# Short and unread products put between runs of 256-column and 512-column products on the tensor engine

## The chip, the cores and the metric

The kernel runs on one core of one Trainium2 chip. The metric is the device time of one launch in microseconds (us). A core has a tensor engine (PE, with its weight loads shown apart as PEld), a vector engine (DVE), a scalar engine (ACT), GpSimd (POOL), a sync engine (SP) that here only issues transfers, and 16 DMA engines.

## The reference

One layer of a hybrid block on 256 latent tokens and 256 context tokens of width 2048, all in float32:

```
mod = silu(c) @ w_ada + b_ada;  shift, scale, gate = split(mod, 3)
h  = rmsnorm(x) * (1 + scale) + shift            # and hc likewise from ctx
xa, za, xb, zb, cv, cg, zc, gl = split(h @ w_in) # widths 7 x 1024 and 3 x 2048
ya = bidirectional gated linear scan of conv4(xa), latents starting from the context's last state
yb = (mean over windows 2, 4, 8, 16 - itself) @ w_pool, per group of 256 channels
yc = silu(layernorm(conv31(cv * sigmoid(cg)))) @ w_pwc + b
t  = sum over k of sigmoid(gl_k) * ((y_k * silu(z_k)) @ w_bout_k)
out = rmsnorm(x + gate * (t @ w_out + b_out)) * final_g
```

Of the context only its `xa` is computed. Nearly all the arithmetic is the products with `w_in`, `w_bout`, `w_pwc` and `w_out`.

## The kernel before

Weights come in pieces of 1 MB (128 partitions of 2048 float32) through three slots. A piece is split into a high part (ACT, L84) and a low part (DVE, L85 through the helper at L210), both of the type float32r, in two halves of 1024 columns each; four buffers of each part let the splits run up to two pieces ahead. The tokens were split in the same way before (`hH`, `hL`). A float32 product is then three float32r products: high by high, high by low, low by high.

`steps` (L297 to L348) is a fixed list of work, one piece of weights each, and sets the order of everything: "xa" and then groups of "xb" and "zb" with the pooling, "cv" and "cg", "gl" and "bout" pairs, "za", "zc", "pwc", and at the end "out". In a step of all kinds but "out", `columns` (L243) takes the weights as the stationary operand, 128x128 at a time, and the tokens as the moving one, 256 columns wide (512 in "xa", where context tokens are taken along): sixteen times L249 and L250 in turn, then sixteen times L253. That is 48 products a step, each with a weight load of its own. "out" (L1065) takes tokens as the stationary operand and 512 columns of weights as the moving one.

Between steps, `Background` emits pieces of elementwise chains into the program, by an estimate of the vector engine's load. Some of them have products of their own, which so come to stand between the runs of `columns`:

- `products` in `lru` (L584): six products of 512 columns for the recurrent gates, through `mm3` (L239 to L241);
- `pool_end` (L808): twelve products of 256 columns of the pooling mixer, also through `mm3`;
- the two sums of the layer norm, 256 columns in plain float32 (L731, L745), and the four of the gate chunks, 512 columns in plain float32 (L940). A plain float32 product shows as two products in the trace.

PE works through all of this in the order in which it is written. Results go to a ring of six banks of PSUM (`bank`) or one of two (`small_bank`).

Of the kernel before, what the change touches and what calls it, by code (L numbers as in the profile page):

```python
# [23 lines left out]

# column offsets inside the packed per-channel vectors
V_G, V_BSH, V_BSC = 0, 16, 32
# [6 lines left out]

# arena offsets (float32 per partition)
A_SQ0, A_XT, A_H, A_S, A_RAW = 0, 8192, 16384, 17408, 17920
# [11 lines left out]
class Feed:  # L47
    """Weight pieces of 8 KB per partition: loaded ahead into slots, and split into two float32r parts."""

# [41 lines left out]
class Background:  # L91
    """Elementwise chains cut into small steps that fill the vector engine between weight splits.

    A chain is a list of named generators that run one after another. Each yields None after what it has just
    emitted, "S" where the next part has to wait for the next weight piece, or a function that says whether the
    next part may be emitted (in a tuple where that is only better so)."""

# [7 lines left out]
    def _step(self, chain):  # L105
        """Emits the next part; False if it can't be emitted yet."""
        if chain["until"] is not None:
            if not chain["until"]():
                return False
            chain["until"] = None  # L110
        try:
            r = next(chain["parts"][0][1])
        except StopIteration:
            self.done.add(chain["parts"].pop(0)[0])
            if not chain["parts"]:
                self.chains.remove(chain)
            return True
        chain["soft"] = isinstance(r, tuple)
        if chain["soft"]:
            r = r[0]  # L120
        if callable(r):
            chain["until"] = r
        return r != "S"
# [22 lines left out]
def hybrid_block_kernel(  # L146
# [91 lines left out]
    def mm3(ps, sh, sl, mh, ml, start, stop):  # L238
        T.matmul(ps, sh, mh, start=start, stop=False)  # L239
        T.matmul(ps, sh, ml, start=False, stop=False)  # L240
        T.matmul(ps, sl, mh, start=False, stop=stop)  # L241

    def columns(jobs):  # L243
        """Sums over k of weights (stationary) times tokens (moving) in three float32r products each; those
        with the low part of the weights come last, so that it may be late. A job: output, high and low parts
        of the weights per k, high and low parts of the tokens per k."""
        for ps, wh, wl, mh, ml in jobs:
            for k in range(len(wh)):
                T.matmul(ps, wh[k], mh[k], start=k == 0, stop=False)  # L249
                T.matmul(ps, wh[k], ml[k], start=False, stop=False)  # L250
        for ps, wh, wl, mh, ml in jobs:
            for k in range(len(wh)):
                T.matmul(ps, wl[k], mh[k], start=False, stop=k == len(wh) - 1)  # L253

    def tiles128(parts):
        """The 128-column tiles of a split piece, high and low."""
        return [[part[i][:, P * k:P * (k + 1)] for part in parts for k in range(8)] for i in range(2)]

    def rsqrt_newton(o, v, tmp, r):
        """o = 1/sqrt(v): square root, reciprocal, one Newton step."""  # L260
        A.activation(r, v, AF.Sqrt)
        recip(r, r)
        tt(tmp, r, r, ALU.mult)
        tt(tmp, tmp, v, ALU.mult)
        ts(tmp, tmp, -0.5, 1.5)
        tt(o, tmp, r, ALU.mult)

    feed = Feed(nc, whp, wlp)

    # order of the weight pieces  # L270
    main_slots = [(f"m{i}", raws[:, i, :]) for i in range(3)]
# [25 lines left out]
    steps = []  # L297
# [57 lines left out]
    with tc.manual_schedule():  # L355
# [1 line left out]
        cin = sml[:, 0:32]  # L357
# [60 lines left out]
        def keep_warm(n):  # L418
            """Products that nothing reads: the tensor engine's clock halves when it has been idle."""
            for _ in range(n):  # L420
                T.matmul(warm, ones, xT[:, 10, :], start=True, stop=True)

# [1 line left out]
        fold = ar[:, A_XS:A_XS + 512]  # L424
# [35 lines left out]

# [1 line left out]
        xa_ps = [bank() for _ in range(6)] + [small_bank() for _ in range(NXA - 6)]  # L462
# [18 lines left out]

# [1 line left out]
        xap = [ar[:, A_XAP + 518 * t:A_XAP + 518 * (t + 1)].rearrange("p (s l) -> p s l", s=2) for t in range(8)]  # L483
# [12 lines left out]
        gth = [ar[:, A_GTH + 512 * i:A_GTH + 512 * (i + 1)] for i in range(2)]  # L496
        # context halves of the split modulated tokens, free after xa: products' operands of the branches
        cH, cL = hH[:, :, 256:512], hL[:, :, 256:512]
# [11 lines left out]

# [1 line left out]
        nsp, tsp, brh, bih = sml[:, 96:112], sml[:, 112:128], sml[:, 128:144], sml[:, 144:160]  # L512

        def prep():
            """softplus(-lam) = max(-lam, 0) + log1p(exp(-|lam|)); log1p(e) = 2 atanh(e / (2 + e))."""
            lam = vt[:, V_LAM:V_LAM + 16]
# [31 lines left out]
        def conv_a(pr):  # L548
            """Two heads: depthwise convolution of width 4, then the two parts of the result."""
            hd = (2 * pr, 2 * pr + 1)  # L550
# [21 lines left out]
        def lru():  # L572
# [11 lines left out]
            def products(h, d):  # L584
                i = h % 2
                for g in range(2):
                    ps = small_bank()
                    w = slice(128 * g, 128 * (g + 1))
                    mm3(ps.rearrange("p (s l) -> p s l", s=2), wH[:, d, w], wL[:, d, w],
                        uH[:, 2 * i:2 * i + 2, :], uL[:, 2 * i:2 * i + 2, :], True, True)  # L590
                    pss[g] = ps
                if d == 1:
                    lru_at["mm"] += 1
# [128 lines left out]
        def layer_norm():  # L722
# [7 lines left out]
            ps = bank()  # L730
            T.matmul(ps[:, 0:256], ones, tree[:, 0:256], start=True, stop=True)  # L731
            A.activation(mu, ps[:, 0:256], AF.Copy, scale=1.0 / 1024)
            yield "S"
# [10 lines left out]
            ps = bank()  # L744
            T.matmul(ps[:, 0:256], ones, tree[:, 0:256], start=True, stop=True)  # L745
            ts(v, ps[:, 0:256], 1.0 / 1024, EPS)
            A.activation(r, v, AF.Sqrt)
# [32 lines left out]

# [1 line left out]
        G.memset(ar[:, A_XAP:A_XAP + 4144], 0.0)  # L782
# [15 lines left out]
        def silu_parts(ps):  # L798
            """(1 + tanh(z / 2)) z, twice silu(z)."""
            th = take("th", th_t)  # L800
# [7 lines left out]
        def pool_end(g):  # L808
# [4 lines left out]
            for j in range(2):  # L813
                for k in range(2):
                    mm3(ps[:, 256 * j:256 * (j + 1)], wH[:, k, 128 * j:128 * (j + 1)],
                        wL[:, k, 128 * j:128 * (j + 1)], pH[:, k, :], pL[:, k, :], k == 0, k == 1)
            for j in range(2):
                t = 2 * g + j
# [53 lines left out]
        def merge_end(k, j):  # L872
            """Two channel tiles of a branch into the sum; after the last branch, half the sum in two parts."""
            a = acc[:, j, :]
# [29 lines left out]
        def gate_chunk(n):  # L904
            """The gate on every partition: silu(c) times the weight rows of each partition, then the sum over
            the partitions; and x + gate * b_out."""
            c = slice(512 * n, 512 * (n + 1))
# [31 lines left out]
            ps = bank()  # L939
            T.matmul(ps, ones, g, start=True, stop=True)  # L940
            A.copy(g, ps)
            yield "S"
# [28 lines left out]
        def finish(t, halves):  # L971
            """The last chunk of a token tile, then the RMS norm over its rows; the first three chunks are
            multiplied by final_g already."""
            var, r, tmp = [sml[:, 16 + 4 * t + i:17 + 4 * t + i] for i in range(3)]
# [25 lines left out]

# [1 line left out]
        first, later, post = [], [], []  # L1002
        step_no = [0]
        avail = load["V"]
        for kind, key, item, q in steps:
# [34 lines left out]
            elif kind == "bout":  # L1040
# [12 lines left out]
                later.append((si + 1, lambda k=k, j=j: merge_end(k, j)))  # L1053
            elif kind == "out":
                if q == 0:
                    if key == 0:
# [8 lines left out]
                def out_mm(t, ps, lo, hi, qs, low):  # L1065
                    """One token tile: tokens stationary, weights moving; the low part of the weights last."""
                    tk = slice(P * t, P * (t + 1))
# [60 lines left out]
def _layout(inputs):  # L1128
    """Arrays in the order in which the kernel reads them: permutations, slices and concatenations only."""
    f = {k: np.asarray(v, dtype=np.float32) for k, v in inputs.items()}  # L1130
# [58 lines left out]
```

## Time and profile before

| | |
|---|---|
| median of 3 runs | 991.86 us (988.95 to 993.12) |
| span of the profiled execution, first to last instruction | 990.5 us |
| own time of the profiled execution, around the span | not given by the profile |
| PE busy | 965.3 us, 97% |
| PE weight loads busy | 893.6 us, 90% |
| DVE busy | 743.6 us, 75% |
| ACT busy | 493.0 us, 50% |
| DMA | 220.70 MB, mean 223 GB/s |

The profile is one execution. Busy shares are averages over the span; PE products are pipelined, so the busy time of one (from its start to its modelled end) is longer than the distance to the start of the next, and how fast PE works is read from the starts. The tensor engine's granted clock is shown as PEclk, 1.00 being the full 2.4 GHz. The first 163 us are the modulation and "xa"; from there to 892 us stand the steps of `columns` with 256 columns; the rest is "out".

### The profile page before, as it was taken

To read this page: it belongs to the slowest core of one execution; us is meant where nothing else is said; L and a number is where in the kernel's file an instruction comes from. 1 tells how busy PE (TensorE), PEld (TensorE's weight loads), DVE (VectorE), ACT (ScalarE), POOL (GpSimd) and SP (SyncE) were. 2 spreads that over 40 slices of the span, in tenths; PEclk is the share of its full clock that TensorE was granted. 3 is DMA by queue.
4 is the path that set the end of the run, shared out by engine and by line. 5 is a ranking of instruction groups with operands and counts; after the bars stand their busy time and mean duration, and the time that the engine had idled before them with its cause. 6 is when DMAs were issued, how large, how long until landed. Compare 5 with 4: busy or idle time off the path is not lost.

```text
span 990.5 us, 18090 instructions
## 1 busy us (share of the span) xinstructions
PE 965.3 (97%) x7528; PEld 893.6 (90%) x7528; DVE 743.6 (75%) x1143; ACT 493.0 (50%) x641; POOL 40.6 (4%) x74
## 2 busy tenths in 40 slices
PE   4999999999999999999999999999999999999996
PEld 1566668999999999999999999999999999998885
DVE  5445456866976775889899899896756788998864
ACT  4212226566656767674444533444565464454442
POOL 0000010000100000000000000000002111101000
PEclk9999999999999999999999999999999999999998
DMA  9897854544545555444555545555468789878652
GB/s 373 322 418 313 359 194 162 211 171 167 181 163 182 182 181 178 174 171 170 203 181 176 200 178 191 193 173 175 169 216 342 256 301 331 326 249 303 214 178 85
DMA packets 34722, 220.70 MB, mean 223 GB/s; under 512 B 4128, under 2 KB 4272, under 8 KB 11856
## 3 DMA queue, kind: packets, MB, share of 16 engines
q1 hardware_dynamic: 28080, 195.28, 54.1%
q0 software_dynamic: 6560, 24.26, 7.2%
q8 instruction: 59, 0.97, 0.4%
q14 instruction: 23, 0.19, 0.1%
HBM read 217.43 MB, written 2.10 MB: 222 GB/s over the span
## 4 chain that ended last, share of the span: by engine, by line
PE 96%; DVE 2%; ACT 1%; DMA 1%; issue 0%; ACTq 0%; SPq 0%; DVEq 0%
PE acc L253 24%; PE acc L250 24%; PE acc L249 24%; PE sm L390 3%; PE acc L239 3%; PE acc L1075 3%; PE acc L1077 3%; PE acc L1078 3%; PE acc L240 2%; PE acc L241 2%; DVE ar L210 1%; PE sm L240 1%; PE sm L239 1%; PE sm L241 1%; DMA ar<-in_xt_dram 1%; PE sm L399 0%
## 5 line engine op out<-in xcount | busy, mean ns | idle before, releaser
L249 PE MATMUL acc<-hH,wh 128*128 128x256 f32 (+1 forms) x2000 | 479.2, 282 | 0.0
L250 PE MATMUL acc<-hL,wh 128*128 128x256 f32 (+1 forms) x2000 | 477.7, 281 | 0.0
L84 ACT CAST wh<-raws 128x1024 fp32r<-128x1024 f32 (+1 forms) x288 | 297.8, 1048 | 274.8 <-PE acc L250 186.6
L210 DVE TENSOR_TENSOR wl<-raws,wh 128x1024 fp32r<-128x1024 f32 (+1 forms) x288 | 339.6, 1217 | 120.9 <-issue 58.5
L250 PEld LDWEIGHTS acc<-hL,wh 128*128 128x128 f32 x2000 | 378.0, 189 | 2.1 <-issue 0.7
L249 PEld LDWEIGHTS acc<-hH,wh 128*128 128x128 f32 x2000 | 377.5, 189 | 2.1 <-issue 0.7
L253 PE MATMUL acc<-hH,wl 128*128 128x256 f32 (+1 forms) x2000 | 260.3, 281 | 0.0
L253 PEld LDWEIGHTS acc<-hH,wl 128*128 128x128 f32 x2000 | 245.8, 189 | 0.7
L221 DVE SCALAR_TENSOR_TENSOR ar<-ar,vt 128x256 f32<-128x256 f32 (+1 forms) x264 | 115.2, 501 | 0.0
L210 DVE TENSOR_TENSOR ar<-ar 128x512 f32<-128x512 f32 (+6 forms) x136 | 87.3, 664 | 7.9 <-ACT ar L430 6.2
L221 DVE SCALAR_TENSOR_TENSOR ar<-ar,sc 128x512 f32<-128x512 f32 x64 | 48.0, 750 | 17.5 <-DMA ar<-in_w_gate_dram 16.1
L235 ACT CAST hH<-ar 128x256 fp32r<-128x256 f32 (+1 forms) x68 | 31.5, 491 | 54.2 <-DVE ar L217 46.9
L210 DVE TENSOR_TENSOR hL<-ar,hH 128x256 fp32r<-128x256 f32 (+1 forms) x76 | 39.5, 546 | 23.1 <-ACT hH L235 23.1
L1077 PE MATMUL acc<-wh,hH 128*128 128x512 f32 (+1 forms) x144 | 51.8, 369 | 0.0
L1078 PE MATMUL acc<-wh,hL 128*128 128x512 f32 (+1 forms) x144 | 51.3, 366 | 0.0
L239 PE MATMUL acc<-hH,wh 128*128 128x512 f32 x96 | 42.7, 445 | 1.2 <-ACT hH L235 1.2
L215 DVE TENSOR_SCALAR sml<-sm,vt 128x2 f32<-128x2 f32 x16 | 3.5, 219 | 50.8 <-PE sm L399 50.8
L240 PE MATMUL acc<-hL,wh 128*128 128x512 f32 x96 | 38.6, 403 | 0.3 <-DVE hL L210 0.2
L241 PE MATMUL acc<-hH,wl 128*128 128x512 f32 x96 | 38.4, 400 | 0.0
L239 PEld LDWEIGHTS acc<-hH,wh 128*128 128x128 f32 x96 | 18.2, 190 | 16.1 <-issue 12.0
L1075 PE MATMUL acc<-wl,hH 128*128 128x512 f32 (+1 forms) x144 | 32.1, 366 | 0.0
L1078 PEld LDWEIGHTS acc<-wh,hL 128*128 128x128 f32 x144 | 27.0, 188 | 4.8 <-issue 0.2
(136 smaller groups left out, 649.8 us busy)
## 6 DMA issues: line engine op xcount, KB each, us to landing
raws<-in_w_br_dram SPq DMA_DIRECT2D x49, 1024.0 KB, 4.9
raws<-in_w_gl_dram SPq DMA_DIRECT2D x48, 1024.0 KB, 4.9
raws<-in_w_bout_dram SPq DMA_DIRECT2D x24, 1024.0 KB, 4.9
raws<-in_w_ada_dram SPq DMA_DIRECT2D x16, 1024.0 KB, 8.9
ar<-in_w_ada_dram SPq DMA_DIRECT2D x16, 1024.0 KB, 8.3
ar<-in_w_gate_dram POOLq DMA_DIRECT2D x32, 512.0 KB, 6.6
raws<-in_w_out_dram SPq DMA_DIRECT2D x16, 1024.0 KB, 5.0
ar<-in_w_xa_dram SPq DMA_DIRECT2D x5, 896.0 KB, 11.5
```

Of the source, the lines that this page charges most:

```text
L84: self.nc.scalar.copy(h[:, 0:w], src)
L210: V.tensor_tensor(out=o, in0=a, in1=b, op=op)
L221: V.scalar_tensor_tensor(o, a, s, b, op0=op0, op1=op1)
L239: T.matmul(ps, sh, mh, start=start, stop=False)
L240: T.matmul(ps, sh, ml, start=False, stop=False)
L241: T.matmul(ps, sl, mh, start=False, stop=stop)
L249: T.matmul(ps, wh[k], mh[k], start=k == 0, stop=False)
L250: T.matmul(ps, wh[k], ml[k], start=False, stop=False)
L253: T.matmul(ps, wl[k], mh[k], start=False, stop=k == len(wh) - 1)
L1075: T.matmul(ps, H, wl[:, w], start=False, stop=kt == KT - 1)
L1077: T.matmul(ps, H, wh[:, w], start=kt == 0, stop=False)
L1078: T.matmul(ps, Lo, wh[:, w], start=False, stop=False)
```

## The change

`columns` gets a lead-in: where the last products on PE were 512 columns wide (`recent["pe"] == "wide"`) and its own are 256 wide, it first issues one product of 64 columns with the same weights and tokens as its first product, into the first 64 columns of the same bank. The first product of the run starts the accumulation anew, so that nothing of the lead-in is left. A new helper `wide` issues one product of 512 columns of tokens by tokens into a bank that nobody reads, and notes that PE was left wide; it is called behind the pool group's products, behind both sums of the layer norm, and behind the sums of the gate chunks as long as "out" hasn't begun. The gates' `products` note it too. Comments and docstrings are taken out, so line numbers move: L249, L250 and L253 become L265, L266 and L269, L731 becomes L748, L745 L763 and L940 L960.

```diff
+    recent = {"pe": "wide"}
+
+    def wide(ps):
+        T.matmul(ps, hH[:, 2, 0:128], hH[:, 0:2, 0:256], start=True, stop=True)
+        recent["pe"] = "wide"
+
+    def lead_in(job):
+        ps, wh, _, mh, _ = job
+        if recent["pe"] == "wide" and ps.shape[-1] == 256:
+            T.matmul(ps[:, 0:64], wh[0], mh[0][:, 0:64], start=True, stop=True)
+        recent["pe"] = "wide" if ps.shape[-1] == 512 else "columns"
+
     def columns(jobs):
+        lead_in(jobs[0])
         for ps, wh, wl, mh, ml in jobs:
...
                     pss[g] = ps
+                recent["pe"] = "wide"
                 if d == 1:
...
             T.matmul(ps[:, 0:256], ones, tree[:, 0:256], start=True, stop=True)
+            wide(small_bank())
             A.activation(mu, ps[:, 0:256], AF.Copy, scale=1.0 / 1024)
...
             T.matmul(ps[:, 0:256], ones, tree[:, 0:256], start=True, stop=True)
+            wide(small_bank())
             ts(v, ps[:, 0:256], 1.0 / 1024, EPS)
...
                         wL[:, k, 128 * j:128 * (j + 1)], pH[:, k, :], pL[:, k, :], k == 0, k == 1)
+            wide(bank())
             for j in range(2):
...
             T.matmul(ps, ones, g, start=True, stop=True)
+            if "gate" not in recent:
+                wide(small_bank())
             A.copy(g, ps)
...
             elif kind == "out":
+                recent["gate"] = True
                 if q == 0:
```

On PE, at the last visit of the recurrent gates' products (at 432 us in the profile before), the order before is as follows. Names stand as out<-in, `sm` is a bank of the small ring, `acc` one of the other, `wh` and `wl` the parts of a piece of weights, and the last word is partitions by moving columns.

```order
L253 MATMUL acc_4035<-hH,wl_1_4029 128x256 x8
L239 MATMUL sm_4158<-hH 128x512
L240 MATMUL sm_4158<-hL,hH 128x512
L241 MATMUL sm_4158<-hH,hL 128x512
L239 MATMUL sm_4162<-hH 128x512
L240 MATMUL sm_4162<-hL,hH 128x512
L241 MATMUL sm_4162<-hH,hL 128x512
L249 MATMUL acc_4182<-hH,wh_0_4097 128x256
L250 MATMUL acc_4182<-hL,wh_0_4097 128x256
```

The run of 256-column products begins straight behind the six. Now, on PE at the same place:

```order
L269 MATMUL acc_4060<-hH,wl_1_4054 128x256 x8
L239 MATMUL sm_4184<-hH 128x512
L240 MATMUL sm_4184<-hL,hH 128x512
L241 MATMUL sm_4184<-hH,hL 128x512
L239 MATMUL sm_4188<-hH 128x512
L240 MATMUL sm_4188<-hL,hH 128x512
L241 MATMUL sm_4188<-hH,hL 128x512
L255 MATMUL acc_4208<-hH,wh_0_4122 128x64
L265 MATMUL acc_4208<-hH,wh_0_4122 128x256
L266 MATMUL acc_4208<-hL,wh_0_4122 128x256
```

One product of 64 columns, with the weights of the next, has come between; the rest stands as before. On PE at the first sum of the layer norm (682 us), before:

```order
L253 MATMUL acc_6921<-hH,wl_0_6910 128x256 x8
L253 MATMUL acc_6921<-hH,wl_1_6914 128x256 x8
L731 MATMUL acc_7029<-ar,ones 128x256
L249 MATMUL acc_7041<-hH,wh_0_6972 128x256
L250 MATMUL acc_7041<-hL,wh_0_6972 128x256
```

The sum is followed at once by the next step. Now, on PE at the same sum:

```order
L269 MATMUL acc_6948<-hH,wl_0_6937 128x256 x8
L269 MATMUL acc_6948<-hH,wl_1_6941 128x256 x8
L748 MATMUL acc_7056<-ar,ones 128x256
L247 MATMUL sm_7058<-hH 128x512
L255 MATMUL acc_7070<-hH,wh_0_6999 128x64
L265 MATMUL acc_7070<-hH,wh_0_6999 128x256
L266 MATMUL acc_7070<-hL,wh_0_6999 128x256
```

An unread product of 512 columns and one of 64 have come between the sum and the step. In all there are 24 products of 64 columns and 9 unread ones of 512 more on PE; the orders of the other engines are as they were.

## Rows read from the trace of the kernel before

**Rows 1.** The page: span, busy time by engine, chain that ended last.
```profile
span 990.5 us, 18090 instructions
...
PE 965.3 (97%) x7528; PEld 893.6 (90%) x7528; DVE 743.6 (75%) x1143; ACT 493.0 (50%) x641; POOL 40.6 (4%) x74
...
PE 96%; DVE 2%; ACT 1%; DMA 1%; issue 0%; ACTq 0%; SPq 0%; DVEq 0%
PE acc L253 24%; PE acc L250 24%; PE acc L249 24%; PE sm L390 3%; PE acc L239 3%; PE acc L1075 3%; PE acc L1077 3%; PE acc L1078 3%; PE acc L240 2%; PE acc L241 2%; DVE ar L210 1%; PE sm L240 1%; PE sm L239 1%; PE sm L241 1%; DMA ar<-in_xt_dram 1%; PE sm L399 0%
```

**Rows 2.** PE in stretches: us, length, busy (products), PEclk, DMA share, GB/s.
```profile
164.00:190.00 26.00, 26.00 (x232) 1.00 0.60 210
...
434.00:682.00 248.00, 248.00 (x2108) 1.00 0.53 186
684.00:704.00 20.00, 20.00 (x179) 1.00 0.56 187
...
791.00:834.00 43.00, 43.00 (x382) 1.00 0.83 303
...
877.00:891.00 14.00, 14.00 (x126) 1.00 0.67 219
```

**Rows 3.** Timeline, PE: start us, length us, what; a step's last sixteen products.
```profile
708.87 2.05 PE L253 MATMUL acc<-hH,wl 128*128 128x256 f32 x16
...
737.14 2.05 PE L253 MATMUL acc<-hH,wl 128*128 128x256 f32 x16
...
794.40 1.98 PE L253 MATMUL acc<-hH,wl 128*128 128x256 f32 x16
...
805.28 1.98 PE L253 MATMUL acc<-hH,wl 128*128 128x256 f32 x16
```

**Rows 4.** Timeline, PE: the last recurrent-gate products and the run behind.
```profile
432.33 0.40 PE L239 MATMUL sm<-hH 128*128 128x512 f32 x1
...
433.71 0.28 PE L249 MATMUL acc<-hH,wh 128*128 128x256 f32 x1
433.83 0.28 PE L250 MATMUL acc<-hL,wh 128*128 128x256 f32 x1
```

**Rows 5.** Timeline, PE: first pool products, then three of the float32 sums.
```profile
190.96 0.28 PE L239 MATMUL acc<-hH 128*128 128x256 f32 x1
191.08 0.28 PE L240 MATMUL acc<-hL,hH 128*128 128x256 f32 x1
...
682.46 0.60 PE L731 MATMUL acc<-ar,ones 128*128 128x256 f32 x2
...
704.67 0.59 PE L745 MATMUL acc<-ar,ones 128*128 128x256 f32 x2
...
789.90 1.02 PE L940 MATMUL acc<-ar,ones 128*128 128x512 f32 x2
```

**Rows 6.** PE groups by shape: line, what, count, busy us and mean ns.
```profile
L249 PE MATMUL acc<-hH,wh 128*128 128x256 f32 x1984 | 472.9, 281 | 0.0
...
L253 PE MATMUL acc<-hH,wl 128*128 128x256 f32 x1984 | 256.4, 280 | 0.0
```

**Rows 7.** Timeline, weight loads: those of the two-column products and behind.
```profile
142.74 0.30 PEld L399 LDWEIGHTS sm<-sel,ar 128*128 128x128 f32 x2
142.96 0.19 PEld L239 LDWEIGHTS acc<-hH,wh 128*128 128x128 f32 x1
143.07 0.19 PEld L240 LDWEIGHTS acc<-hL,wh 128*128 128x128 f32 x1
```

**Rows 8.** DVE in its busiest stretch: columns as in rows 2.
```profile
450.00:480.00 30.00, 28.23 (x42) 1.00 0.53 189
```

**Rows 9.** Timeline near 857 us, DVE and then PE.
```profile
853.89 3.12 DVE L221 SCALAR_TENSOR_TENSOR ar<-ar,sc 128x512 f32<-128x512 f32 x4 [2.03 <-DMA ar<-in_w_gate_dram]
856.92 2.36 DVE L210 TENSOR_TENSOR wl<-raws,wh 128x1024 fp32r<-128x1024 f32 x2
...
859.65 1.11 PE L253 MATMUL acc<-hH,wl 128*128 128x256 f32 x8
```

## The prediction

> **What bounds the kernel now.** I read the page's busy shares and chain first [rows 1]: the tensor engine (PE) is busy 97% of a span of 990.5 us and the chain that ended last is 96% PE. Three source lines, the products of `columns` at L249, L250 and L253, have 24% of that chain each. So time is gained or lost only by what PE itself does between its first product and its last. The profile gives the executed span and no time around it; the median of the three timed runs is 991.86 us, 1.4 us above the span. I make the sum on the span and add 1.4 us at the end, well inside the 4.2 us over which the three runs lie.
>
> Next I asked for PE in stretches [rows 2]. A window counts every product that touches it, two or three more than start in it. With 2.4 taken off, 164 to 190 us holds a product every 113.3 ns, 684 to 704 the same, 791 to 834 the same, 877 to 891 the same; 434 to 682 holds one every 117.8 ns, 118 below. It is the same instruction, from the same lines, with weights and tokens in the same buffers, and the granted clock is 1.00 in all of these rows, so the clock is not the difference. The timeline shows it without counting [rows 3]: the rows are the last sixteen products of a step, a step being 48 products (16 each of L249, L250, L253). Two fast steps take 805.28 - 794.40 = 10.88 us, 5.44 each; five steps at the slow pace 737.14 - 708.87 = 28.27 us, 5.654 each. PE is never idle in either, so this is a pace, not a wait. It holds from one disturbance to the next, over whatever the other engines do in between: 248 us slow, 43 us fast.
>
> Then I looked at what stands where the pace changes. The fast stretch at 164 follows the last 512-column products of "xa". It ends at the first pool group, whose products start 120 ns apart [rows 5], and everything until 682 is slow. Each of the 16 visits to the recurrent gates' six 512-column products leaves the slow pace behind it (two of them stand straight ahead of pool products); the last one is in [rows 4]. The float32 sums change it over: slow to fast at 682.46, fast to slow at 704.67, slow to fast at 789.90 [rows 5], and by [rows 2] the other two of L940 over again. So the pace is carried along by the stream of products, and reset by the way a run is entered.
>
> **What the fast pace is worth.** L249, L250 and L253 have 1984 products of 256 columns each [rows 6]: 5952, or 124 steps. Fast now are 5 steps from 163.75, 4 from 682.7, 8 from 790.4 and 3 from 875.2: 20. The other 104, at 5.654 - 5.440 = 0.214 us, would give back 22.3 us if all were fast. If instead those 20 steps fell to the slow pace, 4.3 us would be lost. These are the two ends of what the edit can do by the pace.
>
> **What is added.** The order of PE has 33 more instructions and is otherwise the same; the other four engines' orders are the same row for row, as are the DMAs. Nothing is queued differently but what stands behind these 33 on PE, and everything does.
> - 24 lead-in products of 64 columns: one after "xa", 14 behind the gates' products, four behind the pool groups, two behind the layer norm's sums, three behind the gate sums at 789.9, 834.3 and 874.7. None like it runs before. From below: a quarter of a slow product, 118/4 = 29 ns. From above: a whole one, 118 ns. Nearest is the place where products have two columns and only the weight loads take time: four loads from 142.74 to 143.07 start 0.11 us apart [rows 7]. A lead-in loads the same 128x128 weights as the product behind it, so it is bound in that way; I take 0.111 us. 24 x 0.111 = 2.7 us (0.7 to 2.8).
> - 9 unread 512-column products ("wide"), four behind the pool groups, two behind the layer norm's sums, three behind gate sums. Six 512-column products take 433.71 - 432.33 = 1.38 us [rows 4], 0.23 each; 9 x 0.23 = 2.1 us. Their banks are not read, and the vector and scalar engines take the sums ahead of them, so nothing else waits for them. In the pool's case the bank comes from the ring of six and shortens the ring by one place for a step; a bank there is read one or two steps after it is filled, so this should cost nothing, and a wait if it does is far under a step.
>
> So 4.8 us are added for certain (2.7 to 4.9), and -22.3 to +4.3 us hang on the pace: the span would be 973.0 to 999.6 us.
>
> **Which end.** The trace has no 64-column product, so the sum can't be closed from rows; the nearest rows have to decide. Two things speak for the fast end. All of the gates' visits leave PE in the same way (the six products, then 118 ns), so one lead-in that works there will work at every one of them, and it gives 5.654 to 5.440 over the whole of 434 to 682. And in the slow pace a product lasts 4.4 ns longer than in the fast one with the same loads; a product too short to cover its successor's weight load puts the weight load, not the stream, in charge of when the next one starts, and the fast pace (113.3) is the one that stands nearer to loads alone (111). Against it: a float32 sum also interrupts the stream, and it leaves fast and slow alternately. That is why I don't give the fast end more than it gets below, and why the lead-ins behind the sums are the part I trust least: there one 512-column product stands ahead, where the gates have six.
>
> The Trainium skill, TensorE: Matmul & The Clock Gate, section Back-to-back issue gap, gives the gap of two products as columns/2.4 plus 2.5 ns when the clock is full. For 256 columns that is 109 ns, a single value; the trace disagrees, with 113.3 and 118 at a granted clock of 1.00 [rows 2]. By the rule no lead-in could change a pace, and 24 gaps of 29 ns and nine of 216 would add 2.6 us by estimate, 994.5 us as timed.
>
> **What may be late next.** The other engines get 3.8% less time per step. VectorE is busiest from 450 to 480 us, 28.23 of 30 [rows 8], 94%; at the fast pace 97.7%, still under the step. Its split parts are ready many us before they are used there. The tightest place is near 857: VectorE waits 2.03 us for a gate-weight DMA, starts two splits at 856.92 (2.36 us) and PE uses the first at 859.65 [rows 9], about 1.5 us after it is done. From 834 to 875 PE would arrive 38 x 0.038 = 1.4 us earlier. That just fits, and a miss costs under 1 us and perhaps the pace of the few steps up to the next lead-in (7 steps, 1.5 us). I put 1 us on this and on lead-ins that don't catch.
>
> **Forecast.** 990.5 - 22.3 + 4.8 + 1.0 = 974.0 us of span, 975.4 us as timed.
>
> **Rivals.**
> 1. *The lead-in does nothing to the pace.* For it: the pace now lasts through step ends, changes of weights and waits that are over, so it may be set by something that a short product doesn't touch. Against it: runs do come out of 512-column products both ways (163.75 fast, 433.71 slow), so the entry matters. Price: 4.8 us added, nothing back: 996.7 us. The Trainium skill's rule above has the same sign.
> 2. *It works behind the gates' products but not behind the sums.* Ahead of the first sum at 682.46 stand 87 steps, 82 of them slow: 82 x 0.214 = 17.5 us back. The sums then leave PE slow: the 15 steps that are fast there now cost 3.2 us. 991.9 + 4.8 - 17.5 + 3.2 = 982.4 us. For it: the sums switch the pace over, the gates never do. The mirror case, only the sums, gives the other 22 slow steps or 4.7 us, which the added products eat: 992 us.
> 3. *The lead-in enters the slow pace (slower than before).* Place: the first product behind each of the 24. If the load-bound start lands where the gates' entry lands now, the four fast stretches go too: 4.3 us lost on top of 4.8: 1001.0 us. It decides at 163.75, where the run is fast now and is given a lead-in that it doesn't need, and again at 682.7 and 790.4. The alternation behind float32 sums speaks for it, the fast stretch at 163.75 against.
>
> **Chances.** Forecast and its neighbours (972 to 979): 0.58. Rival 2 (979 to 988): 0.16, its mirror within 992 +- 3: 0.05. Rival 1: 0.12. Rival 3: 0.09. What a measurement of this kernel can tell from no change is about 0.5%, 5 us, so faster means under 986.9 and slower over 996.8. Faster: 0.58 + 0.15. Same: the mirror, the edge of rival 2, and half of rival 1, which lies on the border: 0.12. Slower: the other half of rival 1 and rival 3: 0.15. The range for 8 in 10 goes from 971.5 (lead-ins at 29 ns and nothing late make 972.4, and the runs spread) to 997, through rival 1; it leaves out rival 3. The likeliest case alone is 972 to 979.
>
> **What will show it.** Right: in the profile after, the timeline has steps of 5.44 us at 500 and at 720, windows there count a product every 113.3 ns; a 64-column product starts about 0.11 us ahead of the next; the run of 44 steps behind the last gates' visit is fast to its end. The span from 163.75 to the first "out" product shrinks from 728 us to about 711. Wrong: steps of 5.65 us behind a lead-in (rival 1, or rival 3 where 164 to 190 has turned slow too), fast up to the first sum and slow behind it (rival 2), or PE idle in 830 to 890 us with VectorE or a DMA as the releaser.

## The result, and the profile after

| | kernel before | kernel after |
|---|---|---|
| median of 4 runs each | 991.02 us (988.95 to 993.12) | 978.26 us (974.82 to 978.62) |
| ratio after to before | | 0.9864 [0.9838, 0.9889] |
| profiled execution: span | 990.5 us | 973.0 us |
| its own time | not given | 974.82 us |
| end of "xa" to first "out" product, profiled | 728.17 us | 713.83 us |
| in it, `columns` intervals of 112 to 115 ns / of 117 to 119 ns | 951 / 4988 | 5497 / 420 |

The change makes the kernel 1.4% faster, 12.8 us at the medians. The last two rows are worked out from the starts of the 5952 products of `columns` in the two traces; an interval belongs to the fast pace or the slow one as the prediction uses these words (the rest of the 5952 stand at a run's edge).

The page of the kernel after: span, busy time by engine, the chain by engine.
```profile
span 973.0 us, 18156 instructions
...
PE 946.5 (97%) x7561; PEld 876.6 (90%) x7561; DVE 743.3 (76%) x1143; ACT 492.8 (51%) x641; POOL 40.7 (4%) x74
...
PE 95%; DVE 2%; DMA 1%; ACT 1%; issue 0%; SPq 0%; ACTq 0%; DVEq 0%
```
Against [rows 1] PE has 33 products more and is busy 18.8 us less; the other engines' busy times are the same within 0.3 us. Part of the 18.8 us lies ahead of xa's end, where the change touches nothing (see below); in the stretch behind it the time came out of how closely PE's products follow each other.

PE of the kernel after in stretches, columns as in [rows 2]: behind xa, behind the last gates' products, behind the two layer norm sums, behind the first two gate sums.
```profile
162.00:187.00 25.00, 25.00 (x223) 1.00 0.63 220
...
430.00:664.00 234.00, 234.00 (x2067) 1.00 0.55 193
...
668.00:687.00 19.00, 19.00 (x170) 1.00 0.59 197
691.00:768.00 77.00, 77.00 (x682) 1.00 0.75 264
773.00:817.00 44.00, 44.00 (x376) 1.00 0.83 308
820.00:856.00 36.00, 36.00 (x320) 1.00 0.84 294
```
With 2.4 taken off each count, as the prediction did, there is a product every 113.3 ns in 430 to 664, where [rows 2] have 117.8 from 434 to 682, and 113.3 or 113.4 in the other rows but one. The odd row is 773 to 817: 44 us for 373.6 products, 117.8 ns. There the row of before was fast (791 to 834, 43 us for 379.6).

Timeline, PE, of the kernel after: the lead-in behind the last gates' products, where [rows 4] end, and the last sixteen products of two steps, as in [rows 3].
```profile
425.63 0.19 PE L255 MATMUL acc<-hH,wh 128*128 128x64 f32 x1
425.66 0.36 PE L265 MATMUL acc<-hH,wh 128*128 128x256 f32 x1
425.86 0.28 PE L266 MATMUL acc<-hL,wh 128*128 128x256 f32 x1
...
426.09 0.28 PE L266 MATMUL acc<-hL,wh 128*128 128x256 f32 x1
...
724.74 1.98 PE L269 MATMUL acc<-hH,wl 128*128 128x256 f32 x16
...
730.18 1.98 PE L269 MATMUL acc<-hH,wl 128*128 128x256 f32 x16
```
A step is 730.18 - 724.74 = 5.44 us where [rows 3] have 5.654 near 720. The lead-in starts at 425.63 and only 0.03 us later the next product is started, but the one behind that comes 0.20 us later and not 0.11. From the lead-in to 426.09 are 0.46 us for three ordinary products at 0.113 and the lead-in: 0.12 us for it.

Timeline at the first gate sum of the kernel after: PE, then VectorE; the last row is VectorE in the kernel before, ahead of the same sum.
```profile
768.26 1.98 PE L269 MATMUL acc<-hH,wl 128*128 128x256 f32 x16
771.11 1.10 PE L960 MATMUL acc<-ar,ones 128*128 128x512 f32 x2 [0.88 <-issue]
...
767.89 3.12 DVE L221 SCALAR_TENSOR_TENSOR ar<-ar,sc 128x512 f32<-128x512 f32 x4 [1.56 <-DMA ar<-in_w_gate_dram]
...
788.06 1.54 DVE L221 SCALAR_TENSOR_TENSOR ar<-ar,sc 128x512 f32<-128x512 f32 x2 [0.81 <-DMA ar<-in_w_gate_dram]
```
Here PE waits 0.88 us. The profile says "issue", but VectorE's products for this sum (L221) end at 767.89 + 3.12 = 771.01 and the sum starts at 771.11; they had started late because they had waited 1.56 us for the gate weights. A faster PE comes to this place before the DMA does. In the kernel before it did not wait here [rows 5], but only just: VectorE's last products for this sum ended at 788.06 + 1.54 = 789.60, and PE started the sum at 789.90, 0.30 us later.

**Where the 14.3 us of the stretch come from.** 4988 - 420 = 4568 products have gone from 117.78 to 113.33 ns: -20.3 us. The wait adds 0.9. What remains is +5.1 us, and the 33 added products account for it: 24 x 0.12 + 9 x 0.23 = 5.0. Behind the stretch the two profiles are equal (88.74 us from the start of the first "out" product to the start of the last). Ahead of it they are not: it starts at 163.75 us in before and at 160.63 in after, though the change touches nothing there. The starts of all twelve experiments lie between 160.5 and 162.2, so the profiled execution of before was the late one. PE from 17 to 36 us shows where, first of before and then of after; the number behind the count is the granted clock.
```profile
17.00:36.00 19.00, 16.13 (x103) 0.82 0.75 303
```
```profile
17.00:36.00 19.00, 15.74 (x129) 1.00 0.91 360
```
In before the granted clock was at 0.50 for a part of this stretch and PE got through fewer products. These 3.1 us are luck, and they are part of the 17.5 us by which the two spans differ.

### The profile page after: what moved, and what is told of

Same layout as the page of the kernel before. It is cut to its first block, busy times and chain, and to the rows that moved or that the text cites. A ratio compares the mean times of both kernels' runs of the same rounds, so it can differ in the third digit from the quotient of the medians.

```text
span 973.0 us, 18156 instructions
## 1 busy us (share of the span) xinstructions
PE 946.5 (97%) x7561; PEld 876.6 (90%) x7561; DVE 743.3 (76%) x1143; ACT 492.8 (51%) x641; POOL 40.7 (4%) x74
## 4 chain that ended last, share of the span: by engine, by line
PE 95%; DVE 2%; DMA 1%; ACT 1%; issue 0%; SPq 0%; ACTq 0%; DVEq 0%
PE acc L265 24%; PE acc L266 24%; PE acc L269 24%; PE sm L406 3%; PE acc L239 3%; PE acc L1100 3%; PE acc L1098 3%; PE acc L1101 3%; PE acc L240 2%; PE acc L241 2%; PE sm L240 1%; DVE ar L210 1%; PE sm L239 1%; PE sm L241 1%; DMA ar<-in_xt_dram 1%; PE acc L960 0%
## 5 line engine op out<-in xcount | busy, mean ns | idle before, releaser
L265 PE MATMUL acc<-hH,wh 128*128 128x256 f32 (+1 forms) x2000 | 466.8, 278 | 0.0
L266 PE MATMUL acc<-hL,wh 128*128 128x256 f32 (+1 forms) x2000 | 464.6, 277 | 0.0
L265 PEld LDWEIGHTS acc<-hH,wh 128*128 128x128 f32 x2000 | 375.6, 188 | 1.7
L266 PEld LDWEIGHTS acc<-hL,wh 128*128 128x128 f32 x2000 | 375.7, 188 | 0.7
L269 PE MATMUL acc<-hH,wl 128*128 128x256 f32 (+1 forms) x2000 | 253.4, 277 | 0.0
L269 PEld LDWEIGHTS acc<-hH,wl 128*128 128x128 f32 x2000 | 239.5, 188 | 0.7
L221 DVE SCALAR_TENSOR_TENSOR ar<-ar,vt 128x256 f32<-128x256 f32 (+1 forms) x264 | 115.3, 503 | 0.0
L221 DVE SCALAR_TENSOR_TENSOR ar<-ar,sc 128x512 f32<-128x512 f32 x64 | 48.1, 751 | 16.4 <-DMA ar<-in_w_gate_dram 15.0
```

Of the source, the lines that this page charges most:

```text
L221: V.scalar_tensor_tensor(o, a, s, b, op0=op0, op1=op1)
```

## The experiments

Each was run beside the kernel before on the same chip (989.13 to 993.67 us). The times of the sixth and seventh are medians; each of the others is one run.

**1. Lead-ins without the wide products.** All nine calls of `wide` taken out; 15 lead-ins are left (xa, 14 gates' visits).
```
-            wide(small_bank())     # both layer norm sums
...
-            wide(bank())           # pool groups
...
-            if "gate" not in recent:
-                wide(small_bank())
```


> The change without the nine unread 512-column products, and so with 15 lead-ins alone: one behind xa, 14 behind the recurrent gates' products; pool groups and float32 sums have nothing behind them, as in the kernel before. Theory (a lead-in's short stream leaves the weight load in charge of the next start, and the run then holds 113.3 ns whatever the 512-column products did): every run behind a lead-in counts 113.3 ns, every run straight behind a pool group 117.8 until the next lead-in (13 steps, 2.8 us), and the float32 sums go on switching the pace over as before: behind the first layer-norm sum slow, behind the second fast, behind the gate sums slow, fast, slow (15 steps, 3.2 us). From the end of xa to the first out product 713 to 715 us, against 728.2 before and 713.8 with the whole change. Rival (the unread 512-column products do the work and lead-ins only count where they follow them): behind the gates still fast, since those have 512 columns of their own, so the same there. Rival (the pace is set anew by any added product, as a matter of count): no rule, fast and slow mixed behind the 14 visits.

Measured: 976.05 us, stretch 715.09 us, 4760 fast intervals and 1162 slow. PE in stretches: behind a pool group, the gates, the first and the second layer norm sum.
```profile
190.00:206.00 16.00, 16.00 (x138) 1.00 0.55 186
...
440.00:660.00 220.00, 220.00 (x1943) 1.00 0.56 194
...
668.00:690.00 22.00, 22.00 (x189) 1.00 0.56 191
693.00:770.00 77.00, 77.00 (x682) 1.00 0.74 263
```
The lead-ins alone make everything behind the gates fast (113.4 ns from 440 to 660). Without a lead-in the sums only switch the pace: fast before 668, slow behind it (22 us for 186.6 products, 117.9 ns), fast behind the next. The first gate sum is the exception: PE waited 1.7 us ahead of it and the run behind came out fast.

**2. Wide products without lead-ins.**
```
-            T.matmul(ps[:, 0:64], wh[0], mh[0][:, 0:64], start=True, stop=True)
+            pass
```


> The change without the 24 lead-ins: the nine unread 512-column products alone. Theory (the lead-in sets the pace): the 14 runs behind the gates' products count 117.8 ns as before, and so do those behind the pool groups; from the end of xa to the first out product 728 to 731 us (728.2 plus 2.1 for the nine, less or more where a sum's switch comes out the other way). Rival (any 512-column product behind a sum brings the fast pace): the runs behind the five sums at 113.3 ns, 724 to 727 us.

Measured: 987.66 us, stretch 726.86 us. PE in stretches: behind a pool group, the gates, the second layer norm sum, the first two gate sums.
```profile
190.00:205.00 15.00, 15.00 (x135) 1.00 0.54 182
...
440.00:660.00 220.00, 220.00 (x1870) 1.00 0.54 186
...
702.00:780.00 78.00, 78.00 (x690) 1.00 0.73 259
786.00:829.00 43.00, 43.00 (x368) 1.00 0.88 318
832.00:869.00 37.00, 37.00 (x317) 1.00 0.87 313
```
The gates' runs are slow (220 us for 1867.6 products, 117.8 ns), so the lead-in is what turns them. But a 512-column product alone is enough behind the pool groups and the layer norm sums. Behind the first two gate sums it leaves the slow pace (PE waited 0.63 us ahead of the first). So the two edits are not interchangeable, and each place has its own answer.

**3. Other lead-ins.** Five kernels, each with one line changed: 256, 192 or 16 columns, or the 64-column product two, three or four times.
```
-            T.matmul(ps[:, 0:64], wh[0], mh[0][:, 0:64], start=True, stop=True)
+            T.matmul(ps[:, 0:192], wh[0], mh[0][:, 0:192], start=True, stop=True)
...
+            for _ in range(2):
+                T.matmul(ps[:, 0:64], wh[0], mh[0][:, 0:64], start=True, stop=True)
```
256 columns: 

> The change with lead-ins of 256 columns, so the first product of a run issued twice. Theory (a short stream is what matters): such a lead-in is no shorter than the products behind it, the weight load has no time in hand, and the 14 runs behind the gates stay at 117.8 ns; each lead-in costs 0.12 us, from the end of xa to the first out product 731 to 734 us. Rival (one more product of any length changes the pace, as the float32 sums switch it over): the runs behind the gates at 113.3 ns, 713 to 716 us.

192 columns: 

> The change with lead-ins of 192 columns. Theory (load in charge): 192 columns stream in 192/256 of 106 to 113 ns, some 80 to 85, less than the 108 ns that stand between two weight loads behind a lead-in in the trace after, so the load is still in charge and the runs are at 113.3 ns behind every lead-in that gave it before; 713 to 715 us from the end of xa to the first out product. Rival (the number 64 matters, by where in some fixed rhythm its stream ends): other runs, many at 117.8 ns, 718 to 733 us.

16 columns: 

> The change with lead-ins of 16 columns. Theory (any product too short to cover the next weight load): as with 64 columns behind the gates, 14 runs at 113.3 ns, 0.108 us a lead-in; 713 to 716 us from the end of xa to the first out product. Rival (the length sets where the run enters, and 64 and 192 happen to suit): runs behind the gates at 117.8 ns, 720 us or more.

64 columns twice: 

> The change with each lead-in issued twice. Theory (the weight load is in charge behind a short product): the second one changes nothing but 24 x 0.108 = 2.6 us; all 14 runs behind the gates at 113.3 ns; 716 to 718 us from the end of xa to the first out product. Rival (each added product switches the pace over, as a float32 sum does): the runs behind the gates back at 117.8 ns, 733 to 736 us.

Three times: 

> The change with each lead-in issued three times. Read from the runs so far: behind the gates none gives slow, one gives fast, two give slow; and behind xa, where the last product before takes 231 or 236 ns by the run, one lead-in gives fast behind 231 and slow behind 236, and none the reverse. So what counts is the place in a rhythm where a run starts, and each lead-in moves it. Theory A (places in a period of 6.67 ns: fast steps are 17 periods, 113.33 ns; loads alone take 111.1 ns, three of them 50 periods): three lead-ins come back near where none began, the runs behind the gates at 117.8 ns, 740 to 745 us from the end of xa to the first out product. Theory B (two states that each lead-in switches over): three as one, 113.3 ns, 718 to 720 us.

Four times: 

> The change with each lead-in issued four times. Theory A (places in a period, a third of it per lead-in): four as one, the runs behind the gates at 113.3 ns, 721 to 724 us from the end of xa to the first out product, three times 2.6 us more than the change and no more. Theory B (two states that each lead-in switches over): four as two, 117.8 ns, 744 to 749 us.

Measured, with the products that touch 440 to 660 us, where only gates' runs stand (1943 is 113.4 ns each, 1870 is 117.8):

| lead-in | time us | stretch us | 440 to 660 | run behind xa |
|---|---|---|---|---|
| none (experiment 2) | 987.66 | 726.86 | 1870 | fast |
| 256 columns | 995.02 | 732.89 | 1870 | slow |
| 192 columns | 980.93 | 718.90 | 1943 | fast |
| 64 columns (after) | 974.82 | 713.83 | 1943 | fast |
| 16 columns | 979.46 | 718.38 | 1944 | slow |
| 64 columns twice | 1001.62 | 739.76 | 1871 | slow |
| three times | 978.82 | 717.98 | 1944 | slow |
| four times | 986.50 | 725.24 | 1943 | fast |

The times hold more than this pace. PE waits at the first gate sum in all eight, from 0.44 us (three times) to 2.65 us (256 and 16 columns), and other runs differ too: with 192 columns those behind all three gate sums are slow. So the column 440 to 660 is the one to compare.

PE in that stretch, of the kernel with two lead-ins and then of the one with four:
```profile
440.00:660.00 220.00, 220.00 (x1871) 1.00 0.53 185
```
```profile
440.00:660.00 220.00, 220.00 (x1943) 1.00 0.55 192
```
Timeline, PE, of the kernel with two: the lead-ins behind the last gates' products, and the run behind.
```profile
436.56 0.30 PE L256 MATMUL acc<-hH,wh 128*128 128x64 f32 x2
436.70 0.36 PE L266 MATMUL acc<-hH,wh 128*128 128x256 f32 x1
436.90 0.28 PE L267 MATMUL acc<-hL,wh 128*128 128x256 f32 x1
437.02 0.28 PE L266 MATMUL acc<-hH,wh 128*128 128x256 f32 x1
```
Behind the second short product the starts look as they do behind one (0.20 us, then 0.12), and yet the run stays slow to its end. This kills the mechanism that I had argued from: by it two short products put the weight load in charge of the next start as one does, and yet the kernel is slower than before the change. I then held two readings against each other: that each lead-in moves the entry by a third of a period, so that three are as none, or that each one switches the pace over. Three times is fast, which the first did not expect, and four times is fast too, which the second did not. With none to four lead-ins the gates' runs are slow, fast, slow, fast, fast. Both readings fall, and I have no rule for it. What stands is that behind the gates 16, 64 and 192 columns do the same, that 256 acts as none, and that the answer changes with the number. In the kernel with four the remaining loss sits elsewhere: its runs behind the pool groups, the first layer norm sum and the second gate sum are slow.

**4. Lead-ins behind the sums without their wide products.** `wide` issues nothing and only marks the place, so 24 lead-ins stand alone.
```
-        T.matmul(ps, hH[:, 2, 0:128], hH[:, 0:2, 0:256], start=True, stop=True)
```


> The change with its 24 lead-ins but none of the nine unread 512-column products: the lead-in stands straight behind pool groups and float32 sums. Theory (a short product alone does it, whatever stands ahead): all runs at 113.3 ns, save perhaps those behind the gate sums, at 2.1 us less than the change: 711 to 713 us from the end of xa to the first out product. Rival (behind pool groups and sums the 512-column product is what brings the pace, as without any lead-in the runs behind the four pool groups and both layer-norm sums were at 113.4 ns with it): 117.8 ns behind the pool groups and behind some sums, 714 to 718 us.

Measured: 976.54 us, stretch 715.25 us. PE in stretches: behind xa, a pool group, the first gate sum.
```profile
164.00:188.00 24.00, 24.00 (x206) 1.00 0.64 224
191.00:207.00 16.00, 16.00 (x138) 1.00 0.51 170
...
780.00:819.00 39.00, 39.00 (x346) 1.00 0.88 320
```
It mirrors experiment 2: a lead-in alone is enough behind the layer norm sums and the gate sums (here 39 us for 343.6 products, 113.5 ns, though behind the first PE had waited 2.4 us) and fails behind the pool groups (118.0 ns). And the run behind xa is slow here, though nothing ahead of it differs from the kernel after.

The timelines at xa's end show what differs. First the kernel after, then this one (its L254, L264, L268 are L255, L265, L269 of after).
```profile
159.23 1.56 PE L269 MATMUL acc<-hH,wl 128*128 128x512 f32 x6
160.63 0.19 PE L255 MATMUL acc<-hH,wh 128*128 128x64 f32 x1
160.66 0.36 PE L265 MATMUL acc<-hH,wh 128*128 128x256 f32 x1
```
```profile
159.30 1.80 PE L268 MATMUL acc<-hH,wl 128*128 128x512 f32 x7
160.93 0.19 PE L254 MATMUL acc<-hH,wh 128*128 128x64 f32 x1
160.97 0.36 PE L264 MATMUL acc<-hH,wh 128*128 128x256 f32 x1
```
The first row holds six products of 512 columns, the lead-in 160.63 - 159.23 = 1.40 us behind the first of them, and in the second kernel seven in 1.63. In the starts to the ns, the last of them stands 231 ns ahead of the lead-in in the first kernel and 236 ns in the second. That varies from execution to execution of one kernel too: it is 236 in the profile of experiment 7, which is the kernel after again. Over all the traces: at 235 or 236 without a lead-in the run behind is fast (before, experiment 2); at 231 with one it is fast (after, experiment 1, 192 columns); at 235 or 236 with one it is slow (16 columns, experiments 4 to 7); at 231 behind a 256-column lead-in, or behind two of 64, it is slow; at 233 it is slow behind three and fast behind four. So a lead-in does not set the fast pace. As I read it, it moves the place at which the run is entered by some ns, and the pace follows from that place; no run shows that place by itself. Behind the gates the last product stands 225 or 226 ns ahead of the lead-in at all 14 visits of the kernel after, and one lead-in mends all of them.

**5. The first gate sum one step later.**
```
             yield "S"
+            if n == 0:
+                yield "S"
             ps = bank()
             T.matmul(ps, ones, g, start=True, stop=True)
```


> The change with the sum of the first gate chunk (and what hangs on it) one step later in the program. In the trace after, PE stands still for 0.9 us ahead of this sum, since VectorE, late by DMAs of gate weights, has not finished the chunk, and the run behind is at 118 ns for its 384 products. If the wait is what spoils that run: no idle PE there, 113.3 ns behind it, 0.9 + 1.7 us less: 711 us from the end of xa to the first out product. If the entry behind a gate sum comes out either way whether PE waited or not: the 0.9 us go and the 1.7 us may stay, 712.9 us.

Measured: 974.61 us, stretch 712.10 us, and PE no longer waits at that sum. PE behind the first gate sum:
```profile
780.00:817.00 37.00, 37.00 (x329) 1.00 0.90 319
```
37 us for 326.6 products, 113.3 ns, where the kernel after has 117.8. So in this pair the slow pace over 44 us goes with the wait for the gate weights: the same lead-in enters the fast pace when the sum is not held up. That a wait always spoils the run is not shown, and experiment 7 speaks against it. In this profile xa's run was slow (236 ns), which takes 1.1 us back (240 products x 4.44 ns).

**6. At each place the edit that works there.** Lead-in behind the gates, a 512-column product alone behind the pool groups, a lead-in alone behind the sums, and the first gate sum one step later.
```
-            wide(small_bank())                  # layer norm sums
+            recent["pe"] = "wide"
...
             wide(bank())                        # pool groups
+            recent["pe"] = "columns"
...
+            if n == 0:
+                yield "S"
...
-            if "gate" not in recent:            # gate sums
-                wide(small_bank())
+            recent["pe"] = "wide"
```


> At each place what the runs showed to be enough: behind the gates' products the lead-in; behind the pool groups the unread 512-column product alone; behind the float32 sums the lead-in alone; and the first gate sum one step later. Against the change that is 4 lead-ins and 5 unread products less, 4 x 0.12 + 5 x 0.23 = 1.6 us, and the 0.9 us of idle PE and 1.7 us of slow run behind the first gate sum. If the places keep what they showed apart: 709 to 711 us from the end of xa to the first out product, and 4 us less than the change as timed, ratio to before about 0.982. Rival (what stands ahead shifts the entries, so that some place falls to the slow pace): a run or two at 117.8 ns, ratio 0.984 to 0.988.

Measured: 972.74 us, median of 4 runs (971.18 to 974.68), ratio to before 0.9816 [0.9794, 0.9837]; stretch 710.33 us. PE in stretches: behind xa, a pool group, the gates, the second layer norm sum, the first gate sum.
```profile
164.00:188.00 24.00, 24.00 (x206) 1.00 0.64 226
191.00:206.00 15.00, 15.00 (x135) 1.00 0.52 173
...
430.00:664.00 234.00, 234.00 (x2067) 1.00 0.56 193
...
691.00:774.00 83.00, 83.00 (x735) 1.00 0.72 257
779.00:814.00 35.00, 35.00 (x311) 1.00 0.91 320
```
Only the run behind xa is slow (255 slow intervals in all). Against the kernel after the stretch is 3.5 us shorter: 0.9 from the wait, 0.7 from the pace (165 x 4.44 ns), 1.6 from five 512-column products at 0.23 and four lead-ins at 0.12 that are no longer there; 0.3 us are not accounted for. Its median and its stretch are the shortest of all; the one run of experiment 5, 974.61 us, lies at the upper end of its range.

**7. The change once more**, beside the sixth.

> The change itself, beside the version with each place on its own, in five rounds. The step list and the code are the same as in the timed runs, 974.82 to 978.62 us there: ratio to before 0.985 to 0.988. In the profile: the run behind xa fast if xa's last product before the lead-in took 231 ns, slow if 236; idle PE ahead of the first gate sum again, 0.5 to 2.5 us.

Measured: 976.27 us, median of 5 runs (975.78 to 978.42), ratio 0.9850 [0.9831, 0.9869], against 991.47 us. So the sixth kernel is 3.5 us below the changed one on the same chip, with no run of either in the other's range. Timeline at the first gate sum in this profile: PE, then VectorE.
```profile
774.94 2.04 PE L960 MATMUL acc<-ar,ones 128*128 128x512 f32 x2 [3.51 <-issue]
...
777.28 0.56 PE L265 MATMUL acc<-hH,wh 128*128 128x256 f32 x1
...
771.73 3.11 DVE L221 SCALAR_TENSOR_TENSOR ar<-ar,sc 128x512 f32<-128x512 f32 x4 [2.73 <-DMA ar<-in_w_gate_dram]
```
PE in stretches around it and in the run behind: the number behind the count is the granted clock.
```profile
774.90:777.20 2.30, 2.26 (x3) 0.50 0.01 4
...
778.00:780.00 2.00, 2.00 (x20) 1.00 0.91 258
...
780.00:817.00 37.00, 37.00 (x329) 1.00 0.88 326
```
The same wait is 3.51 us long here instead of 0.88, more than the 0.5 to 2.5 expected, and in the 2.3 us behind it the granted clock is 0.50, which is 1.2 GHz. Yet the run behind comes out fast (113.3 ns), where the kernel after, the same program, had 117.8 behind its 0.88 us. So a wait can leave either pace behind it, and what decides is open. Its stretch of 717.32 us comes out of the same account: 4988 - 282 = 4706 products x 4.44 ns = -20.9, +5.0 added, +3.5 wait, and 1.5 left over, which I put down to the products at the half clock. This shows how one kernel can lie 3.5 us apart from itself: the length of a wait for a DMA, the clock behind it, and the paces behind this sum and behind xa. That the three runs of the result at 976.4 to 976.8 us of span differ from the profiled 973.0 for these reasons is likely, but they have no trace.

## Why the prediction was right, and where it was not

The forecast was 975.4 us and a span of 974.0; it came to 978.26 and, in the profile, 973.0.

- **What bounds the kernel, and two paces at a granted clock of 1.00:** right. The edit moved nothing but PE's starts, and steps of 5.654 us became 5.44.
- **The pace, -22.3 us:** the profile has -20.3. Of the missing 2.0, 384 slow products behind the first gate sum are 1.7 us.
- **What is added, 4.8 us:** 5.0 to 5.1. A lead-in costs 0.12 us and not 0.111, a wide product 0.23 as taken from [rows 4].
- **What may be late, 1 us near 857 us:** right in kind and cause (gate weights by DMA, then VectorE, then PE), wrong in place. I took the place near 857 us, with about 1.5 us in hand [rows 9], for the tightest of the profile before. That was a misreading: at the first gate sum only 0.30 us were in hand (the row of before shown with the wait). The place near 857 held and the wait came at that sum, 86 us earlier. In the kernel after it brought more than its own 0.88 us: the lead-in behind it did not catch. I had costed the pace behind a miss at seven steps, 1.5 us, near 857; it was 1.7 us, behind the first sum. In the profile of experiment 7 the wait alone is 3.5 us. This is the term to size larger: the forecast lies 2.9 us below the median, and that wait runs from nothing to 3.5 us over the traces.
- **The span's agreement is partly luck.** Over the stretch I forecast 728 to 711 us, -16.5 by the sum (-22.3 + 4.8 + 1.0); it is -14.3, 713.83 us. The 3.1 us by which the profiled execution of before was late ahead of xa's end, at a lower granted clock, more than made up for it.
- **Why a lead-in works:** wrong. I had put it down to the short stream that leaves the weight load in charge of the next start. Two short products have that too and leave the slow pace, and behind xa one lead-in gives either pace. The forecast held because of the other argument, that all of the gates' visits leave PE in the same way, so that what works at one works at all. That one lead-in works there, and two do not, could not be told from what I had argued: so much was luck.
- **Rival 2** (not behind the sums) was half true for the edits taken singly: a wide product alone fails at two gate sums, a lead-in alone fails behind the pool groups. Together they worked at all but the first gate sum in the kernel after, and at that one too in experiment 7. **Rival 3** pointed at xa, and its mechanism is real there: 1.1 us in the executions in which xa ends 235 or 236 ns ahead. With one lead-in it did not spread: the 14 visits to the gates enter otherwise. With two lead-ins its price was nearly paid: 1001.62 us against the 1001.0 that it gave. **Rival 1** is out by experiments 2 and 3.
- **The rule of the Trainium skill** that the prediction weighed (TensorE: Matmul & The Clock Gate, Back-to-back issue gap: 109 ns for 256 columns) is not met by any stretch here: the 5497 fast intervals of the kernel after are 113.3 ns, at a granted clock of 1.00. But that section of the Trainium skill gives the rule for a product by itself and says that in a stream of weight loads and products both set the spacing. Each product here has a weight load of its own, so the rule was the wrong one to weigh, and these runs do not test it.

## What to carry to other kernels

Where an engine is busy all the time and its granted clock is full, count starts per stretch all the same: the same products may run at two paces, and what decides here is how the run is entered. Try an unread short product at an entry that recurs in the same way many times, and measure each place by itself, since what mends one entry spoils another. When the busiest engine gets faster, look for the first DMA that it overtakes: list every place of the profile before at which it starts right behind work that waited for a DMA, with the time in hand at each (0.30 us here, where I had looked at one with 1.5), and price what the wait does to the work behind it.

## What the runs showed of the hardware that was not expected

- Products of 256 columns with a weight load each have two stable paces at a granted clock of 1.00, 113.3 and 117.8 ns, over hundreds of products (2067 in 234 us in the kernel after, 2108 in 248 us before). In the starts, which the trace gives to the ns, the fast interval is 17 x 6.667 ns and the slow one 53 x 6.667 / 3, a cycle of three products; the pool products' 120 ns are 18 x 6.667. This is a reading of the numbers, and what has the 6.667 ns period is open.
- An unread product of 16, 64 or 192 columns behind the gates' products moves the whole run behind it to the other pace; one of 256 does not, and one of 64 alone does not behind the pool groups.
- A layer norm sum in float32 between two runs switches the pace over (the kernel before, and experiment 1 at 668 and 693 us). With one 512-column product behind it the run came out fast behind both of these sums, with the slow pace ahead of the first and the fast one ahead of the second (experiment 2); with one lead-in it stayed fast behind both (experiment 4).
- After 3.51 us without work the granted clock was 0.50 in the 2.3 us that followed, and the sum's two products took 2.04 us where they took 1.10 in the kernel after; there, behind 0.88 us without work, it was 1.00 (773 to 817 us). The Trainium skill, TensorE: Matmul & The Clock Gate, section What's actually happening, has the clock fall to 1.2 GHz behind an idle time; the trace agrees for the wait of 3.51 us. The length of the wait alone does not decide it: at the same sum the granted clock was 0.50 behind 2.03 us without work (192 columns, 772.7 to 775.7 us) and 1.00 behind 2.41 us (experiment 4, 775.2 to 777.2 us).
